# Other places for a first mix, four heads' token sums, head 15's transposes and two rows' endings in a decoder layer

## The chip, the cores and the metric

The kernel runs on one core of a Trainium2 chip. Its time is the device time of one execution in microseconds (us). The engines are TensorE (PE, with its weight loads as PEld), VectorE (DVE), ScalarE (ACT), GpSimd (POOL) and SyncE (SP), each with a queue of its own that is worked off in order; DMA transfers are issued from SP's, POOL's and ACT's queues.

## The reference

One layer of a decoder trunk over 512 tokens of width 2048, in float32. Two mixers stand side by side: multi-head latent attention (16 heads) and a causal spatial gating unit (SGU, 16 groups of 128 channels). Cut to what matters:

```python
mod = silu(c) @ w_ada + b_ada;  shift, scale, gate = split(mod, 3)
h = rmsnorm(x, attn_norm_g) * (1 + scale) + shift
q_lat, kv_lat, k_rope, z_mla, u, v, z_sgu, g_mla, g_sgu = split_cols(h @ w_in)
...
y_mla = causal_mla_attention(q_nope, q_rope, k_nope, k_rope, v_mla) * silu(z_mla)
y_sgu = u * (tril(w_s) @ rmsnorm(v) + b_s) * silu(z_sgu)     # per chunk of 128 tokens and group
merged = sigmoid(g_mla) * y_mla + sigmoid(g_sgu) * y_sgu
x = x + gate * (merged @ w_out)
out = rmsnorm(x, final_norm_g)
```

## The kernel before

Every large product is made of three matmuls in fp32r: each operand is split into a high part (a cast, on ACT) and a low part (source minus high part, a subtraction on DVE), and PE adds high by high, high by low and low by high in one PSUM bank. So for each weight tile there are a raw load (mostly from SP's queue, some from POOL's), a cast on ACT (`w0h`, `w1h`, `w2h`) and a subtraction on DVE (`w0l`, `w1l`, `w2l`) ahead of PE's matmuls. Products are also made Strassen-fashion: sums and differences of blocks of tokens and of weights are formed by DVE, so that fewer products are needed.

**The slots.** The big input projection for the channels of z, g, u, s and t of all heads runs as a row of slots. In each, PE does 24 matmuls of 128x256 (lines 1523 to 1525). A table by slot, filled with `on(slot, kind, function)`, sets the order of everything else: splits, copies of PSUM (`evacuate`), gates (`gate_op`), loads. `place(slot, us, function)` looks for the next slot with room on DVE. The SGU runs between the slots: `sgu_load`, `bias_load` and `v_load` fetch the spatial weights, the bias and a group's v, `sgu_scale` scales v on ACT (line 1077, four ACTIVATEs), `sgu_mix` does four matmuls (line 1083), `sgu_out` is DVE's. Pair 7 of the groups goes first. The rope tables (`rope_make`) are computed by DVE and ACT from slot 4 on.

**The heads.** After the slots come 16 heads: scores, `softmax` (masks and row maxima on DVE, exponentials on ACT, `normalise` on DVE), `transposes` of the probabilities on PE with a split of the results, `pv`, and `merge_a`, which gates the head's output and later (`finish_late`) splits it into `b{h}` and `g{h}`. For heads 8 to 15 the tokens' left and right halves are also combined ("token sums", tiles u and v, j = h - 8): `sums_first` three DVE operations, `sums_second` two; `sums_out` stores both to DRAM for j < 6, `sums_kept` splits them in place for j = 6, 7. They wait in the list `to_sum`; `sum_late(n)` does the next n entries.

**Head 15 and the output projection.** The output projection is a row of granules: `run_granule(s)` gets the next weight split (`ws`) and issues 12 matmuls of 128x512 (line 1863); its cast is two granules ahead. Its first six granules, 0 to 5, lie inside head 15, between the softmax, the transposes and `pv`, so that PE has work while DVE and ACT do the head. From granule 6 on `at_out(step, function)` hangs the rest on granules: broadcasts of gate rows, token loads and splits, the corners (`keep`, `corner_11` and so on) that put the Strassen sums together, `weigh` (by the final norm's gain), and the rows' sums of squares.

**The tail.** The last product is cut into three (`lasts`: row block 0, and two halves of row block 1). `end_row(n)` scales and writes row block n; `last_row`, `known_sum` and `close_sum` finish rows 0 and 1. Each write is `by_dve` or `by_act`: a scaling on that engine, then a DMA.

## Time and profile before

| | |
|---|---|
| median of 3 runs | 1531.49 us (1530.99 to 1532.06) |
| profiled execution, and its span | 1531.96 us, 1530.2 us |
| busy PE, DVE, ACT, POOL | 1509.8, 1239.3, 823.8, 161.9 us |
| read from and written to HBM | 359.52 MB, 60.64 MB (275 GB/s) |
| DMA packets under 512 B | 17497 of 153590 |

A row of a timeline names the start, the busy time, the engine, the line, the operation with its output and inputs, and in brackets how long the engine was idle before and what released it. Names of tiles are printed without their buffer number. The page is of one execution, whose span is the time from the first to the last record; the other 1.76 us of its time lie around the span.

### The profile page before, as it was taken

To read this page: it belongs to the slowest core of one execution; us is meant where nothing else is said; L and a number is where in the kernel's file an instruction comes from. 1 tells how busy PE (TensorE), PEld (TensorE's weight loads), DVE (VectorE), ACT (ScalarE), POOL (GpSimd) and SP (SyncE) were. 2 spreads that over 40 slices of the span, in tenths; PEclk is the share of its full clock that TensorE was granted. 3 is DMA by queue.
4 is the path that set the end of the run, shared out by engine and by line. 5 is a ranking of instruction groups with operands and counts; after the bars stand their busy time and mean duration, and the time that the engine had idled before them with its cause. 6 is when DMAs were issued, how large, how long until landed. Compare 5 with 4: busy or idle time off the path is not lost.

```text
span 1530.2 us, 27553 instructions
## 1 busy us (share of the span) xinstructions
PE 1509.8 (99%) x10512; PEld 1405.0 (92%) x10512; DVE 1239.3 (81%) x1920; ACT 823.8 (54%) x1438; POOL 161.9 (11%) x195
## 2 busy tenths in 40 slices
PE   9999999999999999999999999999999999999997
PEld 7888988999999999999999999999888888877886
DVE  8989988768788888877778777867888878877676
ACT  4444566555545455454555646555655555545664
POOL 0000011011111111111111111102011111200010
PEclk9999999999999999999999999999999999999999
DMA  9978789888999988898889888888789889989884
GB/s 377 394 265 318 236 245 280 228 206 231 267 260 274 258 248 247 257 264 207 218 241 262 220 248 242 226 207 226 236 259 287 228 235 278 260 213 312 279 263 150
DMA packets 153590, 388.42 MB, mean 254 GB/s; under 512 B 17497, under 2 KB 41841, under 8 KB 149489
## 3 DMA queue, kind: packets, MB, share of 16 engines
q1 hardware_dynamic: 126658, 304.34, 56.8%
q0 software_dynamic: 26656, 82.06, 29.9%
q8 instruction: 82, 1.34, 0.3%
q14 instruction: 50, 0.41, 0.1%
q10 hardware_dynamic: 144, 0.26, 0.0%
HBM read 359.52 MB, written 60.64 MB: 275 GB/s over the span
## 4 chain that ended last, share of the span: by engine, by line
PE 89%; DVE 4%; DMA 4%; ACT 2%; issue 1%; SPq 0%; DVEq 0%; ACTq 0%
PE ps L1525 15%; PE ps L1523 15%; PE ps L1524 15%; PE ps L721 9%; PE ps L189 8%; PE ps L188 8%; PE ps L187 8%; PE ps L1863 7%; PE ps L1708 1%; PE ps L1083 1%; DMA gbc<-gate_row 1%; DMA wraw<-in_w 1%; DMA v_d<-lat 1%; DMA lat<-v_d 1%; DVE mx L1687 1%
## 5 line engine op out<-in xcount | busy, mean ns | idle before, releaser
L1523 PE MATMUL ps<-h,w0h 128*128 128x256 f32 x408 | 113.1, 277 | 1.0 <-DVE lat L175 1.0
L1523 PE MATMUL ps<-h,w2h 128*128 128x256 f32 x408 | 113.8, 279 | 0.0
L1525 PE MATMUL ps<-h,w2l 128*128 128x256 f32 x408 | 112.7, 276 | 0.0
L1524 PE MATMUL ps<-h,w0h 128*128 128x256 f32 x408 | 112.7, 276 | 0.0
L1525 PE MATMUL ps<-h,w0l 128*128 128x256 f32 x408 | 112.7, 276 | 0.0
L1524 PE MATMUL ps<-h,w2h 128*128 128x256 f32 x408 | 112.7, 276 | 0.0
L1523 PE MATMUL ps<-h,w1h 128*128 128x256 f32 x400 | 110.8, 277 | 0.0
L1525 PE MATMUL ps<-h,w1l 128*128 128x256 f32 x400 | 110.4, 276 | 0.0
L1524 PE MATMUL ps<-h,w1h 128*128 128x256 f32 x400 | 110.4, 276 | 0.0
L175 DVE TENSOR_TENSOR w0l<-raw,w0h 128x1024 fp32r<-128x1024 f32 x56 | 68.5, 1223 | 30.2 <-ACT w0h L909 29.4
L887 POOL DMA_DIRECT2D wraw<-in_wh x55 | 49.4, 954 | 378.4 <-DVE w1l L175 147.0
L187 PE MATMUL ps<-h,w1h 128*128 128x512 f32 x218 | 86.6, 397 | 0.0
L189 PE MATMUL ps<-h,w1l 128*128 128x512 f32 x218 | 85.1, 390 | 0.0
L188 PE MATMUL ps<-h,w1h 128*128 128x512 f32 x218 | 85.0, 390 | 0.0
L140 ACT CAST w0h<-wraw 128x1024 fp32r<-128x1024 f32 (+5 forms) x64 | 55.9, 881 | 50.9 <-issue 20.6
L175 DVE TENSOR_TENSOR w1l<-wraw,w1h 128x1024 fp32r<-128x1024 f32 x44 | 53.9, 1224 | 35.0 <-ACT w1h L909 35.0
L140 ACT CAST w1h<-wraw 128x1024 fp32r<-128x1024 f32 (+5 forms) x66 | 53.2, 813 | 50.7 <-issue 17.6
L175 DVE TENSOR_TENSOR w2l<-wraw,w2h 128x1024 fp32r<-128x1024 f32 x46 | 56.3, 1224 | 28.9 <-ACT w2h L909 28.9
L187 PE MATMUL ps<-h,w0h 128*128 128x512 f32 x198 | 78.1, 395 | 0.0
L189 PE MATMUL ps<-h,w0l 128*128 128x512 f32 x198 | 77.7, 392 | 0.2
L1523 PEld LDWEIGHTS ps<-h,w0h 128*128 128x128 f32 x408 | 76.6, 188 | 1.1 <-issue 1.1
L188 PE MATMUL ps<-h,w0h 128*128 128x512 f32 x198 | 77.2, 390 | 0.1
(484 smaller groups left out, 5540.3 us busy)
## 6 DMA issues: line engine op xcount, KB each, us to landing
raw<-in_wh SPq DMA_DIRECT2D x104, 512.0 KB, 6.4
wada<-in_wada SPq DMA_DIRECT2D x31, 1024.0 KB, 7.4
wraw<-in_wh POOLq DMA_DIRECT2D x55, 512.0 KB, 8.3
wraw<-in_wh SPq DMA_DIRECT2D x44, 512.0 KB, 6.5
raw<-in_wh POOLq DMA_DIRECT2D x36, 512.0 KB, 7.3
wraw<-in_wo SPq DMA_DIRECT2D x19, 512.0 KB, 6.1
half<-in_w SPq DMA_DIRECT2D x35, 256.0 KB, 6.2
wraw<-in_w SPq DMA_DIRECT2D x16, 512.0 KB, 8.4
```

Source lines behind the costliest of these rows:

```text
L140: self.nc.scalar.copy(hi[e] if isinstance(hi, list) else hi[:, sl], src)
L175: DVE.tensor_tensor(out=out, in0=in0, in1=in1, op=op)
L187: PE.matmul(ps, ah, bh, start=start, stop=False)
L188: PE.matmul(ps, ah, bl, start=False, stop=False)
L189: PE.matmul(ps, al, bh, start=False, stop=stop)
L721: PE.matmul(psv[key][n], x_[:, tk], w_[:, sl], start=st and m == 0, stop=ch == 7 and m == 2, skip_group_check=True)
L887: q_.dma_start(t, wh[h, n, q // 10 - 1], **eng)
L1083: PE.matmul(ps[:, n], v[:, n], wr[:, q], start=True, stop=True)
L1523: PE.matmul(ps[:, :256], wH[:, cols[c]], xh, start=c == 0 and first, stop=False, skip_group_check=True)
L1524: PE.matmul(ps[:, :256], wH[:, cols[c]], xl, start=False, stop=False, skip_group_check=True)
L1525: PE.matmul(ps[:, :256], wL[:, cols[c]], xh, start=False, stop=c == 7, skip_group_check=True)
L1863: PE.matmul(ps[:, o:o + m], x_[:, tk], w_[:, o:o + m], start=c == 0 and e == 0 and p in opens, stop=c == 7 and e == 2, skip_group_check=True)
```

## The change

Four things are put elsewhere. The first SGU mix (pair 7) is two slots later, its loads at the old place; the rope operations begin one slot later, and head 14's u gate is two slots later. The token sums of j = 4 and 5, which were in heads 13 and 14, go into head 15, with u in the tiles `m1` and `m2` and not in `w2h` and `sig`; those of j = 6 and 7, three entries each now, go one to a step into steps 8 to 13. In head 15, granule 1's split is put ahead of the normalising, the transposes come after granule 4 (before: 3) and `pv` after granule 6 (before: 5). In the tail, `end_row(2)` is at step 50, `end_row(3)` ahead of a corner, and rows 0 and 1 are interleaved with other work; the last write is scaled by ACT.

```diff
-        gate_op(ty, h, res[k, which], s)
+        gate_op(ty, h, res[k, which], s + 2 * ((ty, h) == ("u", 14)))
...
-    sgu_end, s_, e_ = {}, 5, -2
+    sgu_end, s_, e_ = {}, 7, -2
     for p in (7, 0, 1, 2, 3, 4, 5, 6):
-        s_ = max(s_, 5 if p in (0, 7) else base[1 + 5 * p + 1] + 2)
-        on(s_ - 3, LOAD, sgu_load, p)
...
+        s_ = max(s_, 7 if p in (0, 7) else base[1 + 5 * p + 1] + 2)
+        ahead = 5 if p == 7 else 3
+        on(s_ - ahead, LOAD, sgu_load, p)
...
-        s_ += 4
+        s_ = 20 if p == 7 else s_ + 4
...
-        s_ = 4
+        s_ = 5
         for us, f in rope:
...
-    used = [max(sgu_end[7], rope_end) + 3] * 3
+    used = [max(sgu_end[7], rope_end) + 2] * 3
...
-    def softmax(dst, between=None):
+    def softmax(dst, between=None, first=False):
...
-            normalise(2)
+            if not first:
+                normalise(2)
             between()
-        if not between:
+        if first or not between:
             normalise(2)
...
-        if j >= 5:
+        if j >= 6:
             return nt(tp, [P, S], F32, "sig", bufs=3)
+        if j >= 4:
+            return at(("m1", "m2")[j - 4], F32)
...
-                to_sum.append(lambda: (sums_second(j, m, box[0]), sums_out(j, m, box[0])) if j < 6 else sums_kept(j, m, box[0]))
+                if j < 6:
+                    to_sum.append(lambda: (sums_second(j, m, box[0]), sums_out(j, m, box[0])))
+                else:
+                    to_sum.append(lambda: (sums_second(j, m, box[0]), sums_high(j, m, box[0])))
+                    to_sum.append(lambda: sums_low(j, m, box[0]))
...
-            pr_ = softmax(dst, lambda: run_granule(1))
-            run_granule(2)
-            sum_late()
-            run_granule(3)
+            pr_ = softmax(dst, lambda: run_granule(1), True)
+            for n, s in ((0, 2), (1, 3), (2, 4)):
+                run_granule(s)
+                sum_late((1, 2, 0)[n])
...
-            for s in range(4, 6):
-                run_granule(s)
+            run_granule(5)
+            sum_late(1)
+            assert not to_sum
+            run_granule(6)
         finish_late()
-        if h == H - 2:
-            sum_late(1)
...
-            sum_late(1)
+            sum_late(1 if more and h < H - 3 else 0)
...
-    def sums_kept(j, v, u):
-        sums_second(j, v, u)
-        hilo(V[j][:, 0], V[j][:, 1], v)
+    def sums_high(j, v, u):
         U[j] = nt(bp.p, [P, S], F32R, f"b{j}"), nt(ga.p, [P, S], F32R, f"g{j}")
-        hilo(*U[j], u)
+        ACT.copy(V[j][:, 0], v)
+        ACT.copy(U[j][0], u)
+
+    def sums_low(j, v, u):
+        for src, hi, lo in ((v, V[j][:, 0], V[j][:, 1]), (u, *U[j])):
+            tt(lo, src, hi.bitcast(F32), ALU.subtract)
...
-    at_out(6, finish_late)
-    at_out(7, token_load, "V", 5)
-    at_out(8, sum_late, 2)
-    at_out(10, sum_late, 2)
+    at_out(7, finish_late)
+    at_out(8, token_load, "V", 5)
+    for s in (8, 9, 10, 11, 12, 13):
+        at_out(s, sum_late, 1)
...
-        at_out((12, 13, 16, 16, 17, 17)[j], token_split, "V", j)
+        at_out((12, 14, 16, 16, 17, 17)[j], token_split, "V", j)
...
-            s = (14, 17)[e] + n
+            s = (14, 18)[e] + n
             at_out(s, corner_11, s, c, n)
...
+    at_out(50, end_row, 2)
+
-    for s in range(6, len(blocks)):
+    for s in range(7, len(blocks)):
...
     corner_12(52, "a", 0)
-    for n in (2, 3):
-        row_sum_of(n)
-    end_row(2)
+    end_row(3)
     corner_12(52, "a", 1)
     run_todo(53)
-    end_row(3)
...
     known_sum(0, slice(0, 3))
     last_row(0, ps[0], 0, S, 3)
-    close_sum(0, 3)
+    weigh(1, 1)
+    root(0, 3)
+    last_row(1, ps[1], 0, S // 2, 3)
+    DVE.reciprocal(out=rs[0], in_=rs[0])
     by_dve(0, 3, True)
     by_act(0, 0)
     by_dve(0, 1, True)
     by_act(0, 2)
-    last_row(1, ps[1], 0, S // 2, 3)
-    weigh(1, 1)
     known_sum(1, slice(0, 4))
     last_row(1, ps[2], S // 2, S // 2, 4)
-    close_sum(1, 4)
+    root(1, 4)
+    DVE.reciprocal(out=rs[1], in_=rs[1])
     by_dve(1, 3, True)
     by_act(1, 0)
     by_dve(1, 1, queue=ACT)
-    by_dve(1, 2)
+    by_act(1, 2)
```

Tags moved with it, and steps of loads and splits that are one later, are left out. `root` is the first line of the old `close_sum`.

ACT's queue at the first mix, where `wraw` and `raw` are raw weights, `lat` tiles of the slots' results and of v, and the row with `rv` is the scaling of v. Before:

```order
L909 CAST w1h_3516<-raw_285_3396 128x1024
L1077 ACTIVATE lat_289_3404<-lat_289_3404,rv_95 128x128 x4
L1498 ACT_TABLE_LOAD
L1498 ACTIVATE lat_304_3551<-lat_189_1947 128x512
L1027 COPY lat_305_3553<-ps_303_3526 128x256
L909 CAST w0h_3557<-wraw_259_3203 128x1024
L909 CAST w2h_3598<-raw_286_3398 128x1024
L909 CAST w1h_3630<-wraw_263_3232 128x1024
```

And after the change:

```order
L909 CAST w1h_3514<-raw_285_3396 128x1024
L1499 ACT_TABLE_LOAD
L1499 ACTIVATE lat_304_3546<-lat_189_1947 128x512
L1027 COPY lat_305_3548<-ps_303_3521 128x256
L909 CAST w0h_3552<-wraw_259_3203 128x1024
L909 CAST w2h_3586<-raw_286_3398 128x1024
L1077 ACTIVATE lat_289_3404<-lat_289_3404,rv_95 128x128 x4
L909 CAST w1h_3622<-wraw_263_3232 128x1024
```

The scaling has moved behind the table load, the sigmoid, a copy out of PSUM and two casts.

DVE's queue in head 15, from the end of the softmax's masks to the third granule's low part; `mx` are the maxima and sums of the softmax, `lat` and `h` the probabilities, `sig`, `b`, `g` the token sums' tiles. Before:

```order
L182 TENSOR_SCALAR mx_16044<-mx_16044 128x2
L1681 RECIPROCAL mx_16044<-mx_16044 128x2
L182 TENSOR_SCALAR lat_1958_16045<-lat_1958_16045,mx_16044 128x512
L182 TENSOR_SCALAR lat_1959_16046<-lat_1959_16046,mx_16044 128x384
L153 TENSOR_TENSOR w1l_16062<-wraw_146_15788,w0h_16026 128x1024
L1681 RECIPROCAL mx_16044<-mx_16044 128x2
L182 TENSOR_SCALAR h_1473_12861<-h_1473_12861,mx_16044 128x256
L182 TENSOR_SCALAR h_1473_12861<-h_1473_12861,mx_16044 128x128
L153 TENSOR_TENSOR w0l_16085<-wraw_147_15892,w1h_16064 128x1024
L175 TENSOR_TENSOR sig_16103<-b_1712_14371,g_1713_14372 128x512
L175 TENSOR_TENSOR sig_15770<-sig_16103,sig_15770 128x256
```

And after the change:

```order
L182 TENSOR_SCALAR mx_16036<-mx_16036 128x2
L153 TENSOR_TENSOR w1l_16051<-wraw_146_15788,w0h_16018 128x1024
L1682 RECIPROCAL mx_16036<-mx_16036 128x2
L182 TENSOR_SCALAR lat_1957_16037<-lat_1957_16037,mx_16036 128x512
L182 TENSOR_SCALAR lat_1958_16038<-lat_1958_16038,mx_16036 128x384
L1682 RECIPROCAL mx_16036<-mx_16036 128x2
L182 TENSOR_SCALAR h_1473_12861<-h_1473_12861,mx_16036 128x256
L182 TENSOR_SCALAR h_1473_12861<-h_1473_12861,mx_16036 128x128
L153 TENSOR_TENSOR w0l_16077<-wraw_147_15888,w1h_16053 128x1024
L175 TENSOR_TENSOR h_1464_12800<-b_1676_14112,g_1677_14113 128x512
L175 TENSOR_TENSOR sig_15621<-h_1464_12800,sig_15621 128x256
L175 TENSOR_TENSOR h_1464_12800<-h_1464_12800 128x256
```

The low part `w1l` has moved ahead of the reciprocal and the two scalings, and the sums are now those of an earlier head, in another tile.

ACT's queue at the end of the program; `ssy` are the sums of squares, `ry` the rows' roots. Before:

```order
L2135 ACTIVATE sig_17403,ssy_16215<-yb_1994_16236 128x256
L2135 ACTIVATE sig_17410,ssy_16215<-yb_1994_16236 128x256
L2143 ACTIVATE ry_16216<-ssy_16215,ry_16216 128x1
L2048 ACTIVATE ya_1990_16232<-ya_1990_16232,ry_16216 128x512
L2057 DMA out<-ya_1990_16232 128x512
```

And after the change:

```order
L2147 ACTIVATE sig_17408,ssy_16231<-yb_1992_16252 128x256
L2155 ACTIVATE ry_16232<-ssy_16231,ry_16232 128x1
L2060 ACTIVATE ya_1988_16248<-ya_1988_16248,ry_16232 128x512
L2069 DMA out<-ya_1988_16248 128x512
L2060 ACTIVATE yb_1992_16252<-yb_1992_16252,ry_16232 128x512
```

A scaling of 128x512 stands behind ACT's own DMA issue now; DVE's last scaling is gone for it.

## The prediction

> **What bounds the kernel now.** I read the page's busy times first, then the waits of PE, then the timeline around each wait that the change can reach. The page:

> ```profile
> span 1530.2 us, 27553 instructions
> ...
> PE 1509.8 (99%) x10512; PEld 1405.0 (92%) x10512; DVE 1239.3 (81%) x1920; ACT 823.8 (54%) x1438; POOL 161.9 (11%) x195
> ```

> PE is busy for 1509.8 of 1530.2 us, and the change takes no matmul away. So a gain can come only from PE's waits, from matmuls that run long, and from what follows the last one: 20.4 us and the stretched matmuls at most. The waits of PE (us in total, times, longest):

> ```profile
> PE ps L1863 <- DVE w1l L153: 4.5, 3, 2.5
> PE ps L1523 <- ACT lat L1027: 1.4, 1, 1.4
> ...
> PE ps L1523 <- DVE lat L175: 1.0, 1, 1.0
> ...
> PE ps L1708 <- DVE lat L175: 0.6, 1, 0.6
> PE ps L1863 <- DVE w0l L153: 0.4, 1, 0.4
> ```

> L1863 is the output projection, L1523 the slots, L1708 a head's transposes. These five rows sum to 7.9 us. The two left out (L481 and L521) belong to earlier stages, which the diff leaves alone.

> **Part A, the first mix.** The timelines of PE, ACT and DVE there:

> ```profile
> 349.65 1.05 PE L1083 MATMUL ps<-wsr,lat 128*128 128x128 f32 x8
> 352.12 0.38 PE L1523 MATMUL ps<-e,w1h 128*128 128x256 f32 x1 [1.43 <-ACT lat L1027]
> ...
> 356.07 0.36 PE L1523 MATMUL ps<-h,w0h 128*128 128x256 f32 x1 [0.96 <-DVE lat L175]
> ```
> ```profile
> 348.59 1.28 ACT L1077 ACTIVATE lat<-lat,rv 128x128 f32<-128x128 f32 x4 [2.29 <-DMA lat<-v_d]
> 349.89 1.28 ACT L1498 ACT_TABLE_LOAD   x1
> ...
> 351.72 0.35 ACT L1027 COPY lat<-ps 128x256 f32<-128x256 f32 x1
> ```
> ```profile
> 351.84 0.69 DVE L175 TENSOR_TENSOR lat<-lat,lat 128x512 f32<-128x512 f32 x1 [2.06 <-ACT lat L1498]
> 353.06 1.23 DVE L175 TENSOR_TENSOR w0l<-wraw,w0h 128x1024 fp32r<-128x1024 f32 x1 [0.52 <-ACT w0h L909]
> ...
> 355.51 0.41 DVE L175 TENSOR_TENSOR lat<-lat,ps 128x256 f32<-128x256 f32 x1
> ```

> ACT stands 2.29 us for the v tile and then scales it; the table load and the copy that frees PE's bank are queued behind. After the change the table load (1.28) falls into those 2.29 us, the copy is done before PE needs it, and the scale follows the casts of the next weights. The 1.43 goes, and PE runs the slot of 352.12 from 349.65 on; with its length less the wait (356.07 - 0.96 - 352.12, about 3.0) it is through by 352.6. Late next is DVE's copy-back of 355.51. From the start of w0l (353.06) to its end (355.92) are 2.86 us. Freed of its idle 2.06 and 0.52, DVE starts w0l near 350.6, so PE goes on near 353.45: a wait of about 0.9 stays. The mix, 1.05, now stands behind that slot, which makes 354.5 against 356.07: 1.6 won. The ends: 1.43 + 0.96 = 2.4 if both waits go, 0.3 if the moved scale's 1.28 delays a cast that PE needs. I take 1.5.

> Also moved here: the second v load goes behind two raw-weight loads on SP, but its mix comes a slot later too; the rope operations come one slot later, head 14's gate operation two. PE has no wait on any of them in its list, and DVE is idle 19% of the time; without that cover one such operation would cost 0.7, as the row of 351.84.

> **Part B, head 14's softmax.** DVE sums tokens ahead of the masks, and PE's transposes wait 7 us later:

> ```profile
> 1339.86 0.69 DVE L175 TENSOR_TENSOR w2h<-b,g 128x512 f32<-128x512 f32 x1
> ...
> 1341.38 0.29 DVE L175 TENSOR_TENSOR ps<-ps,mask 128x128 f32<-128x128 f32 x1
> ```
> ```profile
> 1348.01 0.30 PE L1708 MATMUL ps<-ident,h 128*128 128x128 f32 x1 [0.58 <-DVE lat L175]
> ```

> The three sums (1341.38 - 1339.86 = 1.52) leave this place, so DVE can come up to 1.52 earlier; PE's scores, which the masks need, probably leave 0.6 of that. It is about the wait: I take 0.5, ends 0 and 0.6.

> **Part C, head 15.** PE's waits and the matmuls behind the long one, then ACT, DVE and two stretches (the columns are the stretch, its length, busy PE, PEld, DVE, ACT and POOL, granted clock, DMA share, GB/s):

> ```profile
> 1359.90 0.50 PE L1863 MATMUL ps<-w0l,b 128*128 128x512 f32 x1 [0.44 <-DVE w0l L153]
> ...
> 1365.41 0.50 PE L1863 MATMUL ps<-w1l,b 128*128 128x512 f32 x1 [2.49 <-DVE w1l L153]
> 1365.74 0.40 PE L1863 MATMUL ps<-w0h,g 128*128 128x512 f32 x1
> ...
> 1366.48 0.63 PE L1863 MATMUL ps<-w0h,g 128*128 128x512 f32 x1
> ...
> 1369.86 0.39 PE L1863 MATMUL ps<-w0l,b 128*128 128x512 f32 x1
> 1370.09 0.39 PE L1863 MATMUL ps<-w1h,g 128*128 128x512 f32 x1
> ...
> 1393.12 0.50 PE L1863 MATMUL ps<-w1l,b 128*128 128x512 f32 x1 [1.04 <-DVE w1l L153]
> ...
> 1399.82 0.50 PE L1863 MATMUL ps<-w1l,b 128*128 128x512 f32 x1 [0.96 <-DVE w1l L153]
> ```
> ```profile
> 1357.54 1.05 ACT L140 CAST w2h<-wraw 128x1024 fp32r<-128x1024 f32 x1 [4.60 <-DMA tokU<-w2h]
> ```
> ```profile
> 1363.21 0.16 DVE L1681 RECIPROCAL mx<-mx 128x2 f32<-128x2 f32 x1
> ...
> 1364.14 1.22 DVE L153 TENSOR_TENSOR w1l<-wraw,w0h 128x1024 fp32r<-128x1024 f32 x1
> ```
> ```profile
> 1365.00:1370.00 5.00, 4.59 (x13) 3.65 (x14) 4.83 (x11) 1.09 (x2) 0.03 (x1) 0.66 0.89 180
> ```
> ```profile
> 1385.00:1400.00 15.00, 13.00 (x57) 10.14 (x56) 12.30 (x20) 7.41 (x10) 0.00 (x0) 1.00 0.98 336
> ```

> The waits have three causes. ACT stood 4.60 us until a token store had read w2h, so a granule's cast and lo part came late; then the masks and the normalising stood ahead of w1l; later, two lumps of token sums did. The new code keeps the sums out of w2h, splits ahead of the normalising, and deals the sums out one piece a step. What the four waits cost: 0.44 + 2.49 + 1.04 + 0.96 = 4.93. A matmul's 0.39 laps over its successor's start by 0.16 (pitch 0.23, rows of 1369.86 and 1370.09), and the first after a wait takes 0.33 to the next, 0.10 more: 4 x 0.26 = 1.04. Behind the long wait eight matmuls start from 1366.48 to 1369.86, 3.38 us, where 8 x 0.23 = 1.84 would do, at a granted clock of 0.66 over that stretch: 1.54. In all 7.5. No such stretch follows the waits of 1.04 and 0.96, so I count it to the long wait, and it goes.

> [...] The rows above speak for the wait as the cause.

> Not all 7.5 comes: from 1385 to 1400 DVE worked 12.30 us beside 13.00 of PE, so with PE's waits gone it is 95% full. Where the V and U casts (ACT) and their lo parts (DVE) alternate, a w1l can be late again, I estimate by 0.5, and at two or three other granules by 0.1 to 0.2. I take 6.5. The ends: 7.5, and 4.0 if the two late waits (2.0 + 2 x 0.26 = 2.5) come back whole and 1.0 more with them. The transposes after one granule more move twelve matmuls of 0.23 ahead of them, the same work in another order; what waited on their results, pv, moves by a granule too. SP issues the stores from other tiles but no more of them.

> **Part D, the tail.**

> ```profile
> 1520.00 0.28 PE L1863 MATMUL ps<-b,V 128*128 128x256 f32 x1
> ```
> ```profile
> 1521.98 0.41 DVE L175 TENSOR_TENSOR sig<-ps,gbc 128x256 f32<-128x256 f32 x1
> ...
> 1523.75 0.16 DVE L2144 RECIPROCAL ry<-ry 128x1 f32<-128x1 f32 x1 [0.90 <-ACT ry L2143]
> 1523.95 0.75 DVE L178 SCALAR_TENSOR_TENSOR yb<-yb,ry,gfb 128x512 f32<-128x512 f32 x1
> 1524.62 0.48 DVE L182 TENSOR_SCALAR ya<-ya,ry 128x512 f32<-128x512 f32 x1
> ```
> ```profile
> 1523.95 0.72 ACT L2048 ACTIVATE ya<-ya,ry 128x512 f32<-128x512 f32 x1 [0.23 <-DVE ry L2144]
> 1525.13 0.39 ACTq L2057 DMA_DIRECT2D out<-ya  x1
> ```
> ```profile
> 1525.63 0.44 SPq L2057 DMA_DIRECT2D out<-yb  x1
> ```

> PE ends at 1520.28, DVE takes the last product at 1521.98, 1.70 later, since other work stands ahead. The change puts rows 2 and 3 and the weighing ahead of PE's end, so DVE takes it at about 1520.35, and the reciprocal comes 1.63 earlier, near 1522.1. Against it: the last write was 1.88 behind the reciprocal (1525.63 - 1523.75); now ACT makes it behind its own DMA issue, which waits for DVE: 0.20 + 0.67 + 0.48 + 0.39 + 0.72 and some 0.08 between are 2.54. The last issue is 1.0 earlier. From it to the end of the span were 4.57, with ACT's issue half a microsecond ahead; now it goes out more alone, so some is won there. I take 1.3, ends 0.3 and 2.0.

> **The sum.** 1.5 + 0.5 + 6.5 + 1.3 = 9.8. The profiled execution took 1531.96 (the span and 1.76 around it), 0.47 over the median: 1522.2 against it, 1521.7 against the median of 1531.49. The lower ends (0.3, 0, 4.0, 0.3) give 4.6, or 1526.9; the upper ones (2.4, 0.6, 7.5, 2.0) 12.5, or 1519.0. A measurement tells some 0.2%, 3.06 us, from no change.

> **The rivals.** *Waits come back in head 15.* DVE at 95% speaks for it, six pieces spread over six steps against. PE would wait for w1l at half a dozen granules by 0.5 to 1: part C gives 2 to 4, the whole 5.3 to 7.3, about 1525.

> *The stretch stays.* If it is not the wait's doing, 1.54 less: 1523.2. For it, that it began 1.07 us after the wait ended; against, that none follows the shorter waits. [...]

> *The change doesn't do it.* DMA share in the stretch to 1400 is 0.98: if raw weights, not DVE, set the pace there, PE waits later for what it now gets sooner, and of the 6.5 of C next to nothing is left; with A and D at their lower ends 0 to 2 remain, 1529.5 to 1531.5. Against it: all four waits name DVE, not a transfer.

> *Slower.* In the steps with keeps, ACT is queued behind a copy that waits for a token tile, and that for DVE's lo part of V; the casts of the next granules stand behind it. A wait as long as 2.49 costs 2.49 + 0.26 + 1.54 = 4.3. Three of them undo the 9.8 and make 1534.6; against it, nothing there is longer than DVE's pieces of 1.6.

> **How the numbers follow.** My case 0.54, waits back 0.22, the stretch stays 0.09, no effect 0.08, slower 0.07. The first three are faster by over 0.2%: 0.85, same 0.08, slower 0.07. The likeliest is 1521.7. The range 1519.0 to 1527.0 takes in the first three cases with the ends of all parts, and leaves out some 0.15 above and a little below.

> **What would show it.** A: no wait of L1523 on ACT's copy near 350 and one near 1 on DVE's copy-back. B: none at head 14's transposes. C: no wait over 0.6 between the first granule and the eighteenth, a granted clock of 1.00 throughout, ACT without a wait for the U store. D: the last SP issue some 5.0 behind PE's last matmul start in place of 5.63. Wrong it would be if the sum of L1863's waits stayed over 2.5, or a wait over 2 stood there and the clock fell behind it.

## The result, and the profile after

The changed kernel takes 1520.80 us (median of 6 runs, 1520.36 to 1521.65) against 1531.24 us before (6 runs, 1529.67 to 1532.06): 0.9934 of it, with a 95% interval of 0.9921 to 0.9947, or 10.4 us less. The forecast was 1521.7. The first lines of the page after:

```profile
span 1518.9 us, 27550 instructions
...
PE 1506.3 (99%) x10512; PEld 1403.9 (92%) x10512; DVE 1238.5 (82%) x1919; ACT 824.6 (54%) x1439; POOL 162.5 (11%) x195
```

The span is 11.3 us shorter. The same matmuls kept PE busy 3.5 us less, of which the 1.54 of the stretched ones are a part; the other 7.8 us were waits of PE and the tail. What PE waits for now:

```profile
PE ps L521 <- ACT w0h L140: 1.1, 1, 1.1
PE ps L1524 <- DVE lat L175: 1.1, 1, 1.1
PE ps L481 <- POOL mask L226: 1.1, 1, 1.1
PE ps L188 <- DVE h L178: 0.3, 1, 0.3
PE ps L1872 <- DVE w1l L153: 0.2, 1, 0.2
PE ps L1710 <- DVE lat L175: 0.2, 1, 0.2
```

The lines have moved by a few: L1872 is the old L1863, L1524 the old L1523, L1710 the old L1708. The 4.5 and 0.4 of the output projection have become 0.2, the 0.6 of the transposes 0.2, the 1.4 on ACT's copy is gone, and the 1.0 on DVE's copy-back stays, as 1.07. That one, and what ACT does ahead of it, in the timelines of PE and ACT after:

```profile
353.78 0.36 PE L1524 MATMUL ps<-h,w0h 128*128 128x256 f32 x1 [1.07 <-DVE lat L175]
...
356.63 1.05 PE L1083 MATMUL ps<-wsr,lat 128*128 128x128 f32 x8
```
```profile
346.74 1.28 ACT L1499 ACT_TABLE_LOAD   x1
...
348.58 0.36 ACT L1027 COPY lat<-ps 128x256 f32<-128x256 f32 x1
```

The table load starts where ACT stood idle before, and the copy is done by 348.94, ahead of PE's need. The mix comes a slot behind the wait.

Where the 11.3 us came from can be read by following the same matmuls through both traces. At the slot of 344 (344.20 before, 344.38 after) the changed execution was 0.18 behind. At a mix 130 us further on it was ahead by 1.30, as these two rows show (before, then after):

```profile
475.96 1.05 PE L1083 MATMUL ps<-wsr,lat 128*128 128x128 f32 x8
```
```profile
474.66 1.05 PE L1083 MATMUL ps<-wsr,lat 128*128 128x128 f32 x8
```

So the stage of part A made 1.48 between these two executions. Up to head 14's scores another 0.32 came that I can place nowhere. At the first granule it was ahead by 2.26 (1356.28 before, the first row below), so B and its neighbours made 0.64. At the last matmul (1520.00 before) it was ahead by 9.66, so C made 7.40, and by the end of the span by 11.3, so D made 1.64 (spans are given to a tenth). The first granule's first matmul and the last one after:

```profile
1354.02 0.45 PE L1872 MATMUL ps<-w1h,b 128*128 128x512 f32 x1
...
1510.34 0.28 PE L1872 MATMUL ps<-b,V 128*128 128x256 f32 x1
```

Two stretches of 48 us that hold the work of head 15, before and then after (columns as in the prediction):

```profile
1356.00:1404.00 48.00, 43.06 (x189) 34.44 (x188) 35.23 (x57) 22.73 (x35) 2.26 (x3) 0.96 0.88 273
```
```profile
1354.00:1402.00 48.00, 47.78 (x220) 39.31 (x219) 40.15 (x67) 25.60 (x39) 2.08 (x3) 1.00 0.97 315
```

PE gets through 220 matmuls where it got through 189, DVE does 4.9 us more, and the DMA moves 315 GB/s in place of 273: over these 48 us neither was at its limit before. The clock is 1.00 throughout. The part of it that does the work of the prediction's stretch from 1385 to 1400:

```profile
1377.50:1390.00 12.50, 12.50 (x57) 10.32 (x56) 11.73 (x18) 5.98 (x8) 0.00 (x0) 1.00 1.00 345
```

The same 57 matmuls take 12.50 us and not 15.00. DVE is 94% full there and the DMA's share is 1.00, and PE waits for neither.

In the tail after, DVE takes the last product 0.31 behind the last matmul's start, the first of the last four writes (256 KB each) leaves at 1513.42 and the last at 1515.00:

```profile
1510.65 0.42 DVE L175 TENSOR_TENSOR sig<-ps,gbc 128x256 f32<-128x256 f32 x1
...
1512.44 0.16 DVE L2170 RECIPROCAL ry<-ry 128x1 f32<-128x1 f32 x1 [0.90 <-ACT ry L2155]
```
```profile
1513.42 0.33 SPq L2069 DMA_DIRECT2D out<-yb  x1
...
1515.00 0.33 SPq L2061 DMA_DIRECT2D out<-yb  x1
```

Before, the first of these four left at 1524.73, ahead of the three issues of 1525.13 to 1525.63:

```profile
1524.73 0.33 SPq L2057 DMA_DIRECT2D out<-yb  x1
```

Against the last matmul's start that is 4.73 before and 3.08 after, 1.65 earlier, as much as the reciprocal (3.75 and 2.10). The last write came only 0.97 earlier (5.63 and 4.66), and yet the span ended 1.64 earlier. From the first of the four to the end it is 5.5 us in both.

### The profile page after: what moved, and what is told of

Its sections match the earlier page's. It is cut to its first block, busy times and chain, and to the rows that moved or that the text cites. A ratio compares the mean times of both kernels' runs of the same rounds, so it can differ in the third digit from the quotient of the medians.

```text
span 1518.9 us, 27550 instructions
## 1 busy us (share of the span) xinstructions
PE 1506.3 (99%) x10512; PEld 1403.9 (92%) x10512; DVE 1238.5 (82%) x1919; ACT 824.6 (54%) x1439; POOL 162.5 (11%) x195
## 4 chain that ended last, share of the span: by engine, by line
PE 92%; DMA 3%; DVE 2%; ACT 1%; issue 1%; SPq 0%; ACTq 0%; DVEq 0%; POOL 0%; POOLq 0%
PE ps L1524 15%; PE ps L1525 15%; PE ps L1526 15%; PE ps L1872 9%; PE ps L721 9%; PE ps L189 8%; PE ps L187 8%; PE ps L188 8%; PE ps L1710 1%; PE ps L1083 1%; DMA wraw<-in_w 1%; DMA g<-g_d 1%; PE ps L1673 1%; PE ps L1672 1%; DMA wraw<-in_wo 0%
## 5 line engine op out<-in xcount | busy, mean ns | idle before, releaser
L1524 PE MATMUL ps<-h,w0h 128*128 128x256 f32 x408 | 113.0, 277 | 1.1 <-DVE lat L175 1.1
L1524 PE MATMUL ps<-h,w2h 128*128 128x256 f32 x408 | 113.9, 279 | 0.0
L1524 PE MATMUL ps<-h,w1h 128*128 128x256 f32 x400 | 110.9, 277 | 0.0
L175 DVE TENSOR_TENSOR w0l<-raw,w0h 128x1024 fp32r<-128x1024 f32 x56 | 68.5, 1224 | 31.0 <-ACT w0h L909 30.1
L140 ACT CAST w0h<-wraw 128x1024 fp32r<-128x1024 f32 (+5 forms) x69 | 61.2, 894 | 55.2 <-issue 19.5
L175 DVE TENSOR_TENSOR w1l<-wraw,w1h 128x1024 fp32r<-128x1024 f32 x44 | 53.9, 1224 | 36.8 <-ACT w1h L909 36.8
L140 ACT CAST w1h<-wraw 128x1024 fp32r<-128x1024 f32 (+5 forms) x65 | 52.1, 809 | 51.6 <-issue 19.9
L175 DVE TENSOR_TENSOR w2l<-wraw,w2h 128x1024 fp32r<-128x1024 f32 x46 | 56.3, 1224 | 28.4 <-ACT w2h L909 28.4
L187 PE MATMUL ps<-h,w0h 128*128 128x512 f32 x198 | 78.1, 394 | 0.0
L1524 PEld LDWEIGHTS ps<-h,w0h 128*128 128x128 f32 x408 | 76.6, 188 | 1.2 <-issue 1.2
L909 ACT CAST w1h<-wraw 128x1024 fp32r<-128x1024 f32 x44 | 46.2, 1050 | 57.9 <-DVE wraw L175 45.9
```

The costliest lines, as they stand in the source:

```text
L140: self.nc.scalar.copy(hi[e] if isinstance(hi, list) else hi[:, sl], src)
L175: DVE.tensor_tensor(out=out, in0=in0, in1=in1, op=op)
L187: PE.matmul(ps, ah, bh, start=start, stop=False)
L909: ACT.copy(hi, src)
L1524: PE.matmul(ps[:, :256], wH[:, cols[c]], xh, start=c == 0 and first, stop=False, skip_group_check=True)
```

## The experiments

Each but the last starts from the changed kernel. The time from the first granule's first matmul to the last matmul was 156.35 to 156.38 us in all six profiles of variants in which nothing new waits there (156.32 in the changed kernel), so this stretch shows a tenth of a us; the whole time cannot, since among these executions the first granule began anywhere from 1353.91 to 1354.78. The medians of the changed kernel and of the three variants that cost nothing (below) lie from 1520.80 to 1521.09; "more" is against 1520.9, the middle of these.

**The first mix at its old place.**

```diff
-    sgu_end, s_, e_ = {}, 7, -2
+    sgu_end, s_, e_ = {}, 5, -2
...
-        ahead = 5 if p == 7 else 3
+        ahead = 3
...
-        s_ = 5
+        s_ = 4
         for us, f in rope:
```

The lines left out put head 14's u gate and the later pairs' slots back too.

> The changed kernel with the first mix, its loads, the rope operations and head 14's u gate at their old places. My theory (ACT's table load and copy behind the scaling of v set PE's wait): the two waits of 1.4 and 1.0 near 350 come back, 1.5 us longer than the changed kernel (1.2 to 1.8), about 1522.3. The rival (the slots catch up later, since PE is bound by weights there anyway): the waits show but the end moves by less than 0.5.

Measured: 1522.27 (5 runs, 1521.08 to 1522.99), about the time expected. But the profiled execution, the fastest of the five, had none of the 1.4: ACT did not wait for v, and its time lies within the changed kernel's own runs. So the number does not show the mechanism, and I ran it again.

> The kernel with the first mix at its old place once more, since its profiled execution was the fastest of five and showed no wait for v at ACT. If the landing of v decides: where ACT waits over 1 us for v, PE waits for the copy and the time is near 1522.5; where v lands early, near 1521. The rival (something else spreads the times): times and ACT's wait for v don't go together.

Measured: 1521.7 (1521.1, 1521.7 and one of 1526.6, which I cannot explain). The profiled one, at 1521.1, again had v early:

```profile
347.22 1.28 ACT L1077 ACTIVATE lat<-lat,rv 128x128 f32<-128x128 f32 x4 [0.16 <-DMA lat<-v_d]
```

ACT waited 0.16 for v where the execution profiled before the change waited 2.29. The changed kernel's gain here is therefore not one number. Where v lands early it is nothing: counted from the slot of 344, the mix of 475 comes 0.32 earlier and 0.02 later in these two profiles than in the changed kernel. Where v lands late it is about 1.5. Two other profiles of kernels with the moved mix show that the new place covers a late v: ACT had to wait for it up to 352.50 in one (the normalising first, below) and 351.94 in the other (the tail in its old order), and PE had no wait on ACT's copy in either:

```profile
352.50 1.28 ACT L1077 ACTIVATE lat<-lat,rv 128x128 f32<-128x128 f32 x4 [0.49 <-DMA lat<-v_d]
```

Over all eight runs of the old place the median is 1522.0, 1.1 more. That the longer of these runs are those with a late v is likely but not shown: none of them was profiled.

**The tail in its old order.**

```diff
-    at_out(50, end_row, 2)
...
-    end_row(3)
+    for n in (2, 3):
+        row_sum_of(n)
+    end_row(2)
     corner_12(52, "a", 1)
     run_todo(53)
+    end_row(3)
...
-    by_act(1, 2)
+    by_dve(1, 2)
```

The lines left out put the weighing and row 1's first half behind row 0's writes again.

> The changed kernel with the tail in its old order, the last write scaled by DVE. My theory (after PE's end the DVE chain sets the time): 1.6 us longer (1.2 to 1.9), DVE takes the last product 1.7 after PE's end in place of 0.3, the last SP issue 5.6 after the last matmul's start. The rival (the last three writes are bound by their transfers): under 0.6.

Measured: 1522.45 (5 runs, 1522.2 to 1523.0), 1.5 more. From the last matmul's start to the end of the span 10.23 us, against 8.56 in the changed kernel and 10.20 before: 1.67, as expected. The first and the last of the last four writes:

```profile
1515.00 0.33 SPq L2069 DMA_DIRECT2D out<-yb  x1
...
1515.90 0.44 SPq L2069 DMA_DIRECT2D out<-yb  x1
```

The last one left 5.63 behind the last matmul (1510.27), in the changed kernel 4.66, 0.97 earlier; that does not account for 1.67. The first left 4.73 behind it, in the changed kernel 3.08: 1.65. The end is 5.5 behind the first in both, though the last leaves 0.90 behind the first here and 1.58 there. So the whole of the gain is the chain up to the first of these writes. What scaling the last write on ACT is worth alone, no run shows.

**The token sums of two heads back home.**

```diff
-        if j >= 6:
+        if j >= 5:
             return nt(tp, [P, S], F32, "sig", bufs=3)
-        if j >= 4:
-            return at(("m1", "m2")[j - 4], F32)
...
-                sum_late((1, 2, 0)[n])
+                sum_late((1, 1, 0)[n])
```

and the two calls of `sum_late` in heads 13 and 14 again; the output projection is L1870 in this kernel.

> The changed kernel with the token sums of j = 4 and 5 at their old places in heads 13 and 14 and in their old tiles; the split ahead of the normalising, the transposes a granule later and the one-a-step pieces stay. My theory (the store of the tile that the next cast needs holds ACT, and DVE behind it): head 14's transposes wait about 0.5 again, ACT stands some 4 us for the store, PE waits 0.4 and then 1.3 to 2 for w1l; with the old 0.26 each that is 2.5 to 3.2 us longer, and 1.5 more if the clock falls after a wait of this length. The rival (the order of the split before the normalising was the cure): 0.5 to 1 longer only, from head 14.

Measured: 1524.43 (5 runs, 1523.83 to 1525.13), 3.5 more. The store holds ACT again, and PE waits in head 14 and twice in head 15:

```profile
1357.00 1.05 ACT L140 CAST w2h<-wraw 128x1024 fp32r<-128x1024 f32 x1 [4.65 <-DMA tokU<-w2h]
```
```profile
1347.44 0.30 PE L1710 MATMUL ps<-ident,h 128*128 128x128 f32 x1 [0.58 <-DVE lat L175]
...
1359.36 0.50 PE L1870 MATMUL ps<-w0l,b 128*128 128x512 f32 x1 [0.50 <-DVE w0l L153]
...
1363.99 0.50 PE L1870 MATMUL ps<-w1l,b 128*128 128x512 f32 x1 [1.57 <-DVE w1l L153]
```

From granule to last matmul 159.08, 2.76 more than in the changed kernel: 0.50 + 1.57 + 2 x 0.26 is 2.59. No matmul ran long behind the 1.57, and the granted clock was 1.00 from 1363.5 to 1370.

**The normalising first, with the store gone.**

```diff
-            pr_ = softmax(dst, lambda: run_granule(1), True)
+            pr_ = softmax(dst, lambda: run_granule(1))
```

> The changed kernel with the two normalisings of head 15 ahead of the third granule's low part again, nothing else. If the store was the cause of the long wait: w1l ends near 1358.9 in the trace where PE needs it at 1359.7, so no wait and no change (within 0.3 us). The rival, the second cause that the prediction named (the normalising ahead of w1l): a wait of 0.5 to 1, with 0.26, 0.8 to 1.3 us longer.

Measured: 1521.00 (5 runs, 1520.22 to 1521.45), 156.37 from granule to last matmul: no change. The rival is wrong: with the store gone the order costs nothing. With the store there the wait was 2.49 in the kernel before and 1.57 in the run above, 0.92 less; that the order made this is likely, but the two also differ in where the transposes and the other sums stand.

**The transposes a granule earlier.**

```diff
-            for n, s in ((0, 2), (1, 3), (2, 4)):
+            for n, s in ((0, 2), (1, 3)):
...
+            run_granule(4)
             run_granule(5)
```

> The changed kernel with head 15's transposes ahead of granule 4 again, pv still behind granule 6. My theory (DVE's and ACT's queues set the waits): the probabilities are normalised by 1359.7 in the trace and the transposes come at 1365 in place of 1367.7, their splits fall behind a low part and a sum on DVE; no wait over 0.3 and no change within 0.3 us. The rival (the extra granule is what gave DVE room): a wait of 0.5 to 1.2 at a granule behind the transposes, 0.7 to 1.5 us longer.

Measured: 1520.85 (6 runs, 1520.51 to 1521.55), 156.35: no change.

**The later sums in lumps.**

```diff
-    for s in (8, 9, 10, 11, 12, 13):
-        at_out(s, sum_late, 1)
+    at_out(8, sum_late, 3)
+    at_out(11, sum_late, 3)
```

> The changed kernel with the six pieces of the token sums of j = 6 and 7 in two lumps of three at steps 8 and 11, and not one a step. My theory (DVE's queue ahead of a low part sets the late waits): a lump is 1.5 + 0.9 + 1.2 and the wait for ACT's casts between, so PE waits about 1 twice, as before, with 0.26 each 2.5 us longer (2 to 4). The rival (raw weights at a DMA share near 1 set the pace there): no wait on DVE, within 0.5 us.

Measured: 1523.82 (5 runs, 1522.47 to 1524.39), 2.9 more. PE waits twice, both times for DVE, and the program's transfers are the same:

```profile
1386.92 0.50 PE L1872 MATMUL ps<-w1l,b 128*128 128x512 f32 x1 [1.49 <-DVE w1l L153]
...
1396.42 0.50 PE L1872 MATMUL ps<-w0l,b 128*128 128x512 f32 x1 [1.04 <-DVE w0l L153]
```

From granule to last matmul 158.74, 2.42 more.

**What a wait does to the clock.** DVE was given idle work behind six steps, so that a low part came late by steps.

```diff
+    scr = nt(dpp, [P, S], F32, "scr")
+    DVE.memset(scr, 0.0)
...
+    for s, n in ((19, 5), (24, 6), (29, 7), (34, 8), (39, 9), (44, 10)):
+        at_out(s, busy_dve, n)      # n times scr = scr + scr
```

> The changed kernel with idle work on DVE (5, 6, 7, 8, 9 and 10 additions of 0.69 on a spare tile) behind steps 19, 24, 29, 34, 39 and 44, to make PE wait for a low part by steps of 0.7, from about 0.5 to some 4 us. My theory: a wait costs itself and 0.26; from some length between 1.6 (no dip seen) and 2.5 (a dip seen) eight or so matmuls of 0.63 follow it. [...]

This kernel ran once (1543.38), for its trace. PE waited 1.55, 1.98, 1.58, 2.40, 4.24 and 4.96 us. Behind the first four no matmul ran long; behind the last two eight and nine of them took 0.56 to 0.79. Over 4 us from 1417, 1433, 1449 and 1465 on, where those four end, the granted clock was 1.00; from 1483.5 and 1504 on, where the 4.24 and the 4.96 end, it was 0.57 and 0.51:

```profile
1465.35 0.50 PE L1872 MATMUL ps<-w1l,b 128*128 128x512 f32 x1 [2.40 <-DVE w1l L153]
...
1483.47 0.50 PE L1872 MATMUL ps<-w0l,b 128*128 128x512 f32 x1 [4.24 <-DVE w0l L153]
```

But the kernel before had lost its clock behind 2.49. So the lengths between came next, one execution each of twice the same kernel (7, 7, 9, 9, 7 and 7 additions; 1544.95 and 1546.73).

> As the run with six stalls, but with 7, 7, 9, 9, 7 and 7 additions, for six waits between 2.4 and 3.4 us, where one wait (2.49) had a stretch of slow matmuls behind it and one (2.40) had none. [...]

> The same kernel a second time. [...]

The waits repeat, the slow matmuls don't. The first execution:

```profile
1418.92 0.50 PE L1872 MATMUL ps<-w0l,V 128*128 128x512 f32 x1 [2.98 <-DVE w0l L153]
...
1435.52 0.50 PE L1872 MATMUL ps<-w1l,b 128*128 128x512 f32 x1 [2.70 <-DVE w1l L153]
...
1452.45 0.50 PE L1872 MATMUL ps<-w0l,b 128*128 128x512 f32 x1 [3.03 <-DVE w0l L153]
...
1469.47 0.80 PE L1872 MATMUL ps<-w1l,b 128*128 128x512 f32 x1 [3.12 <-DVE w1l L153]
...
1488.79 0.79 PE L1872 MATMUL ps<-w0l,b 128*128 128x512 f32 x1 [2.78 <-DVE w0l L153]
...
1507.07 0.50 PE L1872 MATMUL ps<-w1l,b 128*128 128x512 f32 x1 [2.78 <-DVE w1l L153]
```

And the second:

```profile
1419.30 0.80 PE L1872 MATMUL ps<-w0l,V 128*128 128x512 f32 x1 [2.99 <-DVE w0l L153]
...
1437.43 0.50 PE L1872 MATMUL ps<-w1l,b 128*128 128x512 f32 x1 [2.70 <-DVE w1l L153]
...
1454.36 0.80 PE L1872 MATMUL ps<-w0l,b 128*128 128x512 f32 x1 [3.03 <-DVE w0l L153]
...
1474.02 0.80 PE L1872 MATMUL ps<-w1l,b 128*128 128x512 f32 x1 [3.03 <-DVE w1l L153]
...
1492.18 0.50 PE L1872 MATMUL ps<-w0l,b 128*128 128x512 f32 x1 [2.78 <-DVE w0l L153]
...
1508.89 0.50 PE L1872 MATMUL ps<-w1l,b 128*128 128x512 f32 x1 [2.78 <-DVE w1l L153]
```

A matmul of 0.8 in these rows opens a stretch of seven to thirteen slow ones, one of 0.50 none. In the first execution those are the fourth and the fifth wait, in the second the first, the third and the fourth: 2.78 brought them once in four, 2.98 and 2.99 once in two, 3.03 twice in three. So the length alone doesn't decide; what else does, these rows leave open.

The granted clock around the wait of 2.49 in the kernel before, and around the fourth (3.12) and the third (3.03) of the first ladder execution (columns as in the prediction; the first number behind the length is PE's busy time, the third from the end the clock):

```profile
1362.98:1366.39 3.41, 0.98 (x4) 0.85 (x5) 3.31 (x10) 2.86 (x8) 0.82 (x1) 1.00 0.78 181
1366.39:1369.80 3.41, 3.41 (x9) 2.65 (x9) 3.27 (x7) 0.04 (x1) 0.00 (x0) 0.50 0.85 213
```
```profile
1464.90:1468.31 3.41, 1.45 (x7) 0.87 (x5) 3.27 (x6) 2.02 (x3) 0.00 (x0) 1.00 0.54 169
1468.31:1471.72 3.41, 2.25 (x5) 1.84 (x6) 3.38 (x4) 0.00 (x0) 0.00 (x0) 0.50 0.36 82
1471.72:1475.14 3.42, 3.42 (x9) 2.67 (x8) 1.16 (x2) 0.57 (x1) 0.86 (x1) 0.50 0.92 256
```
```profile
1447.83:1451.24 3.41, 1.59 (x8) 0.97 (x6) 3.27 (x6) 1.05 (x1) 0.00 (x0) 1.00 0.29 111
1451.24:1454.66 3.42, 2.21 (x10) 1.83 (x11) 2.29 (x3) 0.00 (x0) 0.00 (x0) 1.00 0.32 89
```

Behind the 2.49 the clock was 0.50 from 1366.39 to 1369.80, 3.41 us, in which PE got through 9 matmuls. Behind the 3.12 it was 0.50 from 1468.31 to 1475.14, 6.83 us; hence the thirteen slow matmuls there. Behind the 3.03 of this execution it stayed at 1.00.

**The last write's order, and two rope operations moved.**

```diff
     s_ = 5
+    spend(7, 0.6)
...
     by_act(1, 0)
-    by_dve(1, 1, queue=ACT)
     by_act(1, 2)
+    by_dve(1, 1, queue=ACT)
```

> The changed kernel with two rope operations of DVE's moved behind the copy-back that PE still waits 1.07 for, and with ACT's last scaling ahead of its own DMA issue in the tail. By my steps: 0.5 less at the mix (two operations of 0.23 with their gaps), and the last issue 0.7 earlier in the tail, though three issues then stand close together: 0.3 to 1.2 us shorter than the changed kernel, about 1520. The rival (the last three writes land one after another whatever their order): 0.5 at most.

Measured: 1521.09 (5 runs, 1520.43 to 1521.19): no gain over the changed kernel, against the 0.3 to 1.2 expected. DVE took 1.87 from w0l's start to the copy-back's, in place of 2.38, as expected, and PE's wait at the mix was 0.55 in place of 1.07; but it was 0.57 and 0.48 in the two profiles with a late v, which leave the rope operations alone, so the fall can't be put down to the edit. In the tail the last write left 0.68 earlier, 3.98 behind the last matmul in place of 4.66, but the span ended 8.61 behind it in place of 8.56:

```profile
1513.87 0.33 SPq L2070 DMA_DIRECT2D out<-yb  x1
1514.30 0.38 SPq L2062 DMA_DIRECT2D out<-ya  x1
1514.77 0.44 SPq L2062 DMA_DIRECT2D out<-yb  x1
```

With ACT's own at 1514.27, four writes leave within 0.9 us, and the rival is right as to the time: the end is 5.5 behind the first of them again, whenever the last leaves. The DMA was full there: from 1514.34 to 1516.34 in the changed kernel its share was 1.01 at 378 GB/s, at which four writes of 256 KB take 2.8 us (an estimate from that rate).

**The kernel before, profiled again.**

> The kernel before, profiled again. Its runs spread over 4 us and more, those of the changed kernel over 1.3. If the slow stretch in head 15 is there in some executions only, this profile may be without it, with the same wait of about 2.5, and some 1.5 us of the loss in head 15 gone; if the wait always brings it, it is there.

Measured: 1530.97 (8 runs, 1529.42 to 1537.14; the profiled one 1529.95). The stretch is there again, and behind the same wait:

```profile
1363.62 0.80 PE L1863 MATMUL ps<-w1l,b 128*128 128x512 f32 x1 [2.50 <-DVE w1l L153]
```

From granule to last matmul 163.52, against 163.72 in the first profile. What was missing was the wait on ACT's copy at the mix, as in the two runs with the mix at its old place. From the slot of 344 to the mix of 475 this execution was 1.75 shorter than the first profile of the same kernel, 0.27 more than the change had won there. So both profiles of the kernel before have the stretch, and v's landing accounts for some 1.7 of the spread of its runs; the rest of it stays open.

## Why the prediction was right

*Part A* (1.5): 1.48 between the two profiled executions, by the chain that was followed, the wait of about 0.9 that stays included (1.07). But the term took one execution for all: by medians it is worth 1.1, and nothing where v lands early, as in the other profile of the kernel before. The prediction should have priced the landing as a range; its row "2.29 <-DMA lat<-v_d" names a transfer. That the size came out is luck to that extent.

*Part B* (0.5): the wait fell from 0.58 to 0.21, so one of 0.2 stayed where none was expected; between the scores and the first granule 0.64 were won. Of the rest 0.23 came at the first transpose: it started 0.46 behind the matmul ahead of it before (1346.34 to 1346.80) and 0.23 after (1344.72 to 1344.95); for that gap the trace names no other engine, so its cause stays open.

*Part C* (6.5): 7.40, of the 7.5 that the four waits and the stretch were worth. The mis-sized term is the 1.0 held back for new waits: one of 0.22 came, at 1401.30. DVE was as full as foreseen (94% in the matching stretch, 95% forecast), but a full DVE did not make a low part late where the sums came one piece a step; the step from "full" to "late" was the wrong one. The causes were three, as said, but not of equal weight. Putting the sums of j = 4 and 5 elsewhere made 2.76; dealing out the later ones 2.42 against lumps of three; the wait's last 0.92 and its stretch of 1.54 hung on that store, probably with the order of normalising. That sums to 7.6, for 7.40; since each was measured with the others in place, and the lumps of the kernel before were other ones, the agreement is rough. The order of normalising alone, and the later transposes, made nothing. The stretch was rightly counted to the wait, but it was not certain: of fourteen waits from 2.49 to 3.12 us, in four profiles, seven brought slow matmuls. The stretch is there in both profiles of the kernel before.

*Part D* (1.3): 1.64. The reciprocal came 1.65 earlier (1.63 expected) and the last issue 0.97 (1.0 expected; the "some 5.0 behind" that was to show D does not agree with that working, which gives 4.63; 4.66 was measured). The step that was wrong is to count the end from the last write: 0.66 was taken off because that write comes later behind the reciprocal, and 0.3 put back because it goes out more alone. The end came 5.5 behind the first of the four writes, so neither term was there, and the 1.65 was won whole.

*The sum.* Between the two profiled executions the span fell by 11.3, 1.5 more than the 9.8. That the median came within 0.9 of the forecast is in part luck: the profiled execution before, with v late, lay 0.7 above the median of its kernel.

*The rivals.* Waits did not come back, and nothing was slower: no wait in the output projection was over 0.22. The DMA was not the pace: its rate rose with PE's (273 to 315 GB/s over those 48 us). The stretch went with its wait: the granted clock was 1.00 from 1354 to 1402. The sum by the rows was right.

## What to carry to other kernels

Where several engines feed a bound one, price each of its waits by what stands ahead in the feeder's queue, and ask for the first cause: here one store of a shared tile held the casts, and without it the order of split and normalising was free. Deal deferrable work out in pieces shorter than the feeder's slack, one per step. Before you count on a wait that ends with a DMA, read a second profile: such a wait may be there in one execution and not in the next (ACT's for v was 2.29 us in one profile of the kernel before, and none in the other). Where the last writes fill the DMA (a share of 1.01 here), count the end from the first of them.

## What the runs showed of the hardware

The span ended 5.5 us behind the first of the last four writes of 256 KB in four profiles (the kernel before, the changed kernel, the old tail, the other order), whether the last of them left 0.9 us behind the first or 1.58.
